# Reordering the first S5 scan: pairs of batches whose steps alternate, and two chains where a batch runs alone

## The chip, the core and the metric

The kernel runs on one core of one Trainium2 chip. The metric is the time of one execution on the device, in microseconds (us). Three runs of the kernel before took 1806.61, 1806.78 and 1822.71 us; the median is 1806.78 us. On the core, TensorE does the matmuls, VectorE and ScalarE the elementwise work, SyncE issues most of the DMAs, and GpSimd does almost nothing here. In the rows TensorE is PE (its weight loads are PEld), VectorE is DVE, ScalarE is ACT, SyncE is SP.

## The reference, cut to what matters

The model is four layers deep over 384 tokens: one sequence of 256 sample tokens and one of 128 prompt tokens, 1024 wide. Layers 0 and 3 are S5 layers, layer 1 is a pooling mixer, layer 2 is attention. An S5 layer projects the normed tokens to `u` and `z` (2048 wide each), drives 128 groups of 64 complex states with `u`, reads the states out, and ends with GELU, a gated linear unit and an output projection:

```
u, z = split(h @ w_in, 2)
for dirn in range(2):                      # forward and backward in time
    bu = einsum('blgc,gpc->blgp', ug, b_bar)
    _, states = associative_scan(_lin_rec, (a, bu), axis=1, reverse=(dirn == 1))
    y = y + einsum('blgp,gcp->blgc', states, c_mat).real
y = gelu(y)
y = y * sigmoid(y @ glu_w + glu_b)
out = (y * silu(z)) @ w_out
```

The scan is a linear recurrence `s[t] = a * s[t-1] + bu[t]` with complex numbers. The sample starts from given states, the prompt from zero, and the prompt's last states are an output.

## The kernel before, in words

**Tiling.** Four tokens are taken as one step of the recurrence, so the sample has 64 steps and the prompt 32. The 128 groups are done in four batches of 32 (`b` = 0 to 3). For one batch, the states of both directions lie on 128 partitions, and a tile `E` of 99 rows of 64 values holds them: rows 0 to 32 are the first half of the sample, rows 33 to 65 the prompt, rows 66 to 98 the second half of the sample. There are two such tiles, so batch 2 uses the tile of batch 0 and batch 3 that of batch 1.

**The scan** (`step`, from L1133). One step of one batch is three VectorE instructions, each of which needs the one before: a product `Pr` (state times the complex factor), a sum `R` of its parts, and an addition of `R` into the next row of `E`. In steps 0 to 31 one instruction covers the first half of the sample and the prompt together (`ns = 2`); here such a step is called wide, and its `Pr` writes 128x256. In steps 32 to 62 it covers the second half of the sample alone (`ns = 1`), a narrow step, whose `Pr` writes 128x128. Step 31 writes into row 66, where the second half of the sample begins. `Pr` and `R` have one buffer for even and one for odd batches.

**What surrounds the scan of a batch.** `u(b)` (L1074) multiplies the tokens with the weights for batch `b` on TensorE (L213), into three PSUM banks that VectorE transposes into a tile `U`; there are three `U` tiles, so `u(3)` writes the one of batch 0. `win(b, qq)` (L1099), four times a batch, makes a weight tile `W` (VectorE products `w`, transposes on TensorE at L910, copies on ScalarE), masks `U` on ScalarE (L1113), multiplies (L1122) and copies the result into `E` (L1125). `mats(q)` (L1222) makes the readout matrices `P` and `M` of a quarter (VectorE products `P`, `t`, TensorE L938, a round trip through DRAM). `out(b, qq)` (L1229) reads a quarter out: two large copies `Eq<-E` on ScalarE (L1185, L1188), matmuls (L1208, L1212), GELU, and a store to `yd`. `P` has four buffers. `z(q)` (L1086), 16 times, is a product for the gate path that only the end of the layer needs (TensorE L204). `fill` runs four pieces of the modulation of later layers (weights `adw` from DRAM, TensorE L99). `glu.early_y` and `glu.early_prod` begin the gated linear unit with what is ready.

**What sets the order.** `run` of `S5Body` (L1234) goes through the batches one after the other. For each it lists tasks by the step ahead of which they are to be written down (`at(step, task)`), then `rec` (L1156) writes down the 63 steps with the tasks between, then the four `out`. This is the order of writing. When the program is built, a planner gives every engine a fixed order of its own: it steps through estimated durations, and gives a free engine the first instruction in the order of writing whose inputs and buffers are ready in that estimate. On the chip every engine goes through its list in order and waits at semaphores. So the order of writing is a priority, not the order that runs. Layer 3 has a class of its own, `S5Skewed` (L1274), whose `phase` already alternates the second half of one batch with the first half of the next.

Of the kernel before, what the change touches and what calls it, by code (L numbers as in the profile page):

```python
# [9 lines left out]
F32 = mybir.dt.float32  # L10
# [1021 lines left out]
class S5Body:  # L1032
# [99 lines left out]

    def step(self, b, i):  # L1133


        n, sb, E = self.n, self.sb, self.Es[b % len(self.Es)]
        Tb = self.Tb[:, :, 32 * b:32 * b + 32].rearrange("p o a r -> p o (a r)")
        P = sb.tile([128, 256], F32, name="Pr", tag=f"Pr{b % 2}")
        R = sb.tile([128, 128], F32, name="R", tag=f"R{b % 2}")
        ns, x = (2, i) if i < 32 else (1, 34 + i)  # L1140
        at = lambda x, d=33: raw_ap(E, 64 * x, [[64 * d, ns], [1, 64]])
        P, R = P[:, :128 * ns].rearrange("p (o s a) -> p o s a", o=2, s=ns), R[:, :64 * ns].rearrange("p (s a) -> p s a", s=ns)
        yield n.tt(P, raw_ap(E, 64 * x, [[0, 2], [33 * 64, ns], [1, 64]]), Tb.unsqueeze(2).broadcast_to([128, 2, ns, 64]), OP.mult)
# [3 lines left out]
        yield n.tt(at(66, -1) if i == 31 else at(x + 1), R, at(x + 1), OP.add)  # L1147

# [6 lines left out]

    def rec(self, b, tasks):  # L1156

        self.begin(b)
        for i in range(63):
            for t in tasks.get(i, ()):  # L1160
                t()
            for _ in self.step(b, i):
                pass
        self.final(b)

# [65 lines left out]
    def run(self, h, fill, glu):  # L1231
# [7 lines left out]
        zs = list(range(16))  # L1239
        for b in range(4):  # L1240
            tasks = {}
            at = lambda i, f, *a: tasks.setdefault(i, []).append(lambda: f(*a))
            if b < 3:
                at(4, self.u, b + 1)
            for qq in range(4):
                if b < 3:
                    at(8 + 14 * qq, self.win, b + 1, qq)
                at(6 + 14 * qq, self.mats, 4 * b + qq)
            for k in range((3, 4, 3, 6)[b]):
                at(62, self.z, zs.pop(0))  # L1250
            if fill:
                for k in range((4, 3, 2, 1)[b]):
                    at(45, fill)
            if b == 3:
                for q in range(8):
                    at(min(62, 30 + 6 * q), glu.early_y, self.wq, q)
                for q in zs:
                    at(62, self.z, q)
                for q in range(2):
                    at(62, glu.early_prod, q)  # L1260
            self.rec(b, tasks)
            for qq in range(4):
                q = 4 * b + qq
                self.out(b, qq)
                if b == 3:
                    for k in range(2, 6):
# [7 lines left out]
class S5Skewed(S5Body):  # L1274

    def phase(self, f, tasks):

        if f < 4:  # L1280
            self.begin(f)
        for i in range(32):
            for t in tasks.get(i, ()):
                t()
            chains = ([self.step(f - 1, 32 + i)] if f and i < 31 else []) + ([self.step(f, i)] if f < 4 else [])
            for _ in range(3):
                for c in chains:
                    next(c)
        if f:
            self.final(f - 1)  # L1290

    def run(self, h, fill, glu):
# [7 lines left out]
        for f in range(5):  # L1300
# [14 lines left out]
            if f == 4:  # L1315
# [9 lines left out]
                for qq in (1, 2, 0):  # L1325
                    at(0, early, qq)
            self.phase(f, tasks)
            for qq in range(4 if f else 0):
# [205 lines left out]
```

## Time and profile before

The profiled execution took 1812.23 us, its span (first to last instruction) is 1810.4 us, and the mean granted TensorE clock is 0.963 of full speed.

| | busy us | share of the span |
|---|---|---|
| PE | 1686.1 | 93% |
| PEld | 1318.4 | 73% |
| DVE | 1254.9 | 69% |
| ACT | 978.3 | 54% |

The shares are averages over stages that differ. The chain of work that ended last lies 72% on PE, 9% on DVE, 9% on ACT and 6% on DMAs. The first S5 scan, which the change touches, begins at 92 us and the readout of its last batch ends at about 480 us.

### The profile page before, as it was taken

To read this page: it belongs to the slowest core of one execution; us is meant where nothing else is said; L and a number is where in the kernel's file an instruction comes from. 1 tells how busy PE (TensorE), PEld (TensorE's weight loads), DVE (VectorE), ACT (ScalarE), POOL (GpSimd) and SP (SyncE) were. 2 spreads that over 40 slices of the span, in tenths; PEclk is the share of its full clock that TensorE was granted. 3 is DMA by queue.
4 is the path that set the end of the run, shared out by engine and by line. 5 is a ranking of instruction groups with operands and counts; after the bars stand their busy time and mean duration, and the time that the engine had idled before them with its cause. 6 is when DMAs were issued, how large, how long until landed. Compare 5 with 4: busy or idle time off the path is not lost.

```text
span 1810.4 us, 29493 instructions
## 1 busy us (share of the span) xinstructions
PE 1686.1 (93%) x10928; PEld 1318.4 (73%) x10928; DVE 1254.9 (69%) x3149; ACT 978.3 (54%) x1588; POOL 5.4 (0%) x16
## 2 busy tenths in 40 slices
PE   4999999998999998999998999999899999899998
PEld 1464454654799977999887885657678778689986
DVE  7699876787476567888867737763439978656435
ACT  2653487636654455655546555642354777754322
POOL 0000000000000000000000000000000000000000
PEclk7999999997899998999998999999999999799999
DMA  8337767654577664655563566732567754567552
GB/s 311 98 119 240 228 182 220 195 180 137 166 252 231 193 205 135 188 162 163 179 218 113 186 205 229 239 127 82 181 226 226 227 182 140 166 232 213 172 165 72
DMA packets 174831, 334.30 MB, mean 185 GB/s; under 512 B 78528, under 2 KB 101856, under 8 KB 174688
## 3 DMA queue, kind: packets, MB, share of 16 engines
q1 hardware_dynamic: 165728, 319.84, 55.6%
q10 hardware_dynamic: 8960, 12.59, 2.1%
q8 instruction: 86, 1.41, 0.3%
q14 instruction: 57, 0.47, 0.1%
HBM read 279.54 MB, written 52.82 MB: 184 GB/s over the span
## 4 chain that ended last, share of the span: by engine, by line
PE 72%; DVE 9%; ACT 9%; DMA 6%; issue 3%; SPq 0%; ACTq 0%; DVEq 0%
PE acc L175 6%; PE acc L177 6%; PE acc L176 6%; PE sp L1122 4%; PE acc L829 4%; PE acc L830 4%; PE acc L831 4%; PE acc L213 3%; PE acc L159 3%; PE acc L160 3%; PE acc L161 3%; PE acc L204 3%; ACT Eq L1188 3%; DMA adw<-in_ada_w 2%; PE adps L99 2%
## 5 line engine op out<-in xcount | busy, mean ns | idle before, releaser
L51 DVE TENSOR_TENSOR wlo<-raw,whi 128x1024 fp32r<-128x1024 f32 (+2 forms) x234 | 281.2, 1204 | 246.3 <-ACT whi L138 229.0
L138 ACT CAST whi<-raw 128x1024 fp32r<-128x1024 f32 x246 | 257.6, 1050 | 315.2 <-PE acc L177 130.0
L51 DVE TENSOR_TENSOR Pr<-E,Tb 128x256 f32<-128x256 f32 (+1 forms) x504 | 173.9, 354 | 9.3 <-ACT E L1131 3.3
L159 PE MATMUL acc<-hh,whi 128*128 128x384 f32 x512 | 177.3, 347 | 0.2
L161 PE MATMUL acc<-hh,wlo 128*128 128x384 f32 x512 | 174.3, 340 | 0.3 <-DVE wlo L51 0.2
L160 PE MATMUL acc<-hl,whi 128*128 128x384 f32 x512 | 174.3, 340 | 0.0
L829 PE MATMUL acc<-y,whi 128*128 128x384 f32 x448 | 152.7, 345 | 8.1 <-ACT y L146 5.8
L831 PE MATMUL acc<-y,wlo 128*128 128x384 f32 x448 | 152.0, 340 | 1.0 <-DVE wlo L51 1.0
L830 PE MATMUL acc<-y,whi 128*128 128x384 f32 x448 | 152.7, 342 | 0.1
L175 PE MATMUL acc<-whi,ph 128*128 128x512 f32 x384 | 152.5, 397 | 0.0
L176 PE MATMUL acc<-wlo,ph 128*128 128x512 f32 x384 | 151.4, 394 | 0.0
L177 PE MATMUL acc<-whi,pl 128*128 128x512 f32 x384 | 151.3, 394 | 0.0
L51 DVE TENSOR_TENSOR E<-R,E 128x128 f32<-128x128 f32 (+1 forms) x504 | 123.1, 254 | 31.5 <-ACT E L1125 25.2
L51 DVE TENSOR_TENSOR R<-Pr 128x128 f32<-128x128 f32 (+1 forms) x504 | 123.7, 255 | 5.8
L159 PEld LDWEIGHTS acc<-hh,whi 128*128 128x128 f32 x512 | 97.1, 190 | 5.2 <-issue 2.0
L204 PE MATMUL acc<-h,raw 128*128 128x384 f32 x256 | 98.8, 516 | 0.0
L161 PEld LDWEIGHTS acc<-hh,wlo 128*128 128x128 f32 x512 | 96.8, 189 | 2.1 <-DVE wlo L51 0.9
L160 PEld LDWEIGHTS acc<-hl,whi 128*128 128x128 f32 x512 | 97.1, 190 | 1.0 <-issue 0.3
L99 PE MATMUL adps<-adw,scond 128*32 128x256 f32 x768 | 70.6, 422 | 27.7 <-DMA adw<-in_ada_w 27.3
L213 PE MATMUL acc<-raw,h 128*128 128x512 f32 x192 | 95.8, 617 | 0.0
L829 PEld LDWEIGHTS acc<-y,whi 128*128 128x128 f32 x448 | 84.6, 190 | 11.6 <-ACT y L146 7.1
L831 PEld LDWEIGHTS acc<-y,wlo 128*128 128x128 f32 x448 | 84.9, 190 | 2.2 <-DVE wlo L51 1.6
(285 smaller groups left out, 3261.6 us busy)
## 6 DMA issues: line engine op xcount, KB each, us to landing
adw<-in_ada_w SPq DMA_DIRECT2D x96, 512.0 KB
raw<-in_s_glu SPq DMA_DIRECT2D x64, 512.0 KB
raw<-in_s_wu SPq DMA_DIRECT2D x48, 512.0 KB
raw<-in_s_wz SPq DMA_DIRECT2D x40, 512.0 KB
raw<-in_s_wo SPq DMA_DIRECT2D x32, 512.0 KB
yq<-yd SPq DMA_DIRECT2D x64, 192.0 KB
lod<-wlo SPq DMA_DIRECT2D x24, 512.0 KB
wlo<-lod SPq DMA_DIRECT2D x24, 512.0 KB
```

The costliest lines, as they stand in the source:

```text
L51: return self.nc.vector.tensor_tensor(out=out, in0=a, in1=b, op=op)
L138: nc.scalar.copy(out=hi, in_=raw)
L159: nc.tensor.matmul(ps, h, xh[:, kk, :ncol], start=i == 0, stop=False)
L160: nc.tensor.matmul(ps, h, xl[:, kk, :ncol], start=False, stop=False)
L161: nc.tensor.matmul(ps, l, xh[:, kk, :ncol], start=False, stop=i == n - 1)
L175: nc.tensor.matmul(ps, xh[:, kk, xs], h, start=kk == 0, stop=False)
L176: nc.tensor.matmul(ps, xh[:, kk, xs], l, start=False, stop=False)
L177: nc.tensor.matmul(ps, xl[:, kk, xs], h, start=False, stop=kk == 2 * nu - 1)
L204: self.nc.tensor.matmul(ps, w[:, k * 128:(k + 1) * 128], x[:, k, :], start=k == 0, stop=k == 7)
L829: self.nc.tensor.matmul(ps, h, y[:, 0, k], start=u == 0 and k == 0, stop=False)
L830: self.nc.tensor.matmul(ps, h, y[:, 1, k], start=False, stop=False)
L831: self.nc.tensor.matmul(ps, l, y[:, 0, k], start=False, stop=u == 1 and k == 7)
```

## The change

`step` gets an argument `part`: with it, a first-half step covers the sample (`part` 0) or the prompt (`part` 1) alone, with `Pr` and `R` buffers of its own. `rec` goes, and `phase`, moved from `S5Skewed` up to `S5Body`, takes its place: it writes down 32 rounds in which the second half of one batch (`second`) and the first half of another (`first`) alternate instruction by instruction. Where there is no `second`, the first half is written as two alternating narrow chains. `S5Body.run` now has six phases: batch 0 alone (two chains), batches 0 and 1 as a pair, the second half of batch 1 alone (one chain), and the same for batches 2 and 3. The tasks are listed anew over 32 rounds a phase. `u(f + 1)` stands at the head of phases 0 to 2, so `u(3)` comes with the second half of batch 1 and no longer with the first half of batch 2. `mats` and `win` stand in the phases of one batch. The 16 `z` were placed 3, 4, 3, 6 over the batches and are placed 2, 4, 2, 2, 4, 2 over the phases; the ten `fill` were 4, 3, 2, 1 and are 2, 2, 2, 2, 1, 1. `S5Skewed` passes its batches to the same `phase` and writes down what it did before.

```diff
-    def step(self, b, i):
+    def step(self, b, i, part=None):
...
-        P = sb.tile([128, 256], F32, name="Pr", tag=f"Pr{b % 2}")
-        R = sb.tile([128, 128], F32, name="R", tag=f"R{b % 2}")
+        c = (b + (part or 0)) % 2
+        P = sb.tile([128, 256], F32, name="Pr", tag=f"Pr{c}")
+        R = sb.tile([128, 128], F32, name="R", tag=f"R{c}")
         ns, x = (2, i) if i < 32 else (1, 34 + i)
+        if part is not None:
+            ns, x = 1, i + 33 * part
...
-    def rec(self, b, tasks):
-
-        self.begin(b)
-        for i in range(63):
+    def phase(self, first, second, tasks):
+
+
+        if first is not None:
+            self.begin(first)
+        for i in range(32):
             for t in tasks.get(i, ()):
                 t()
-            for _ in self.step(b, i):
-                pass
-        self.final(b)
+            chains = [self.step(second, 32 + i)] if second is not None and i < 31 else []
+            if first is not None:
+                chains += [self.step(first, i)] if second is not None else [self.step(first, i, p) for p in range(2)]
+            for _ in range(3):
+                for c in chains:
+                    next(c)
+        if second is not None:
+            self.final(second)
...
-        for b in range(4):
+
+        for f, (first, second) in enumerate(((0, None), (1, 0), (None, 1), (2, None), (3, 2), (None, 3))):
             tasks = {}
-            at = lambda i, f, *a: tasks.setdefault(i, []).append(lambda: f(*a))
-            if b < 3:
-                at(4, self.u, b + 1)
+            at = lambda i, g, *a: tasks.setdefault(i, []).append(lambda: g(*a))
+            if f < 3:
+                at(0, self.u, f + 1)
+            mat, win = ((0, 1), None, (1, 2), (2, 3), None, (3, None))[f] or (None, None)
             for qq in range(4):
-                if b < 3:
-                    at(8 + 14 * qq, self.win, b + 1, qq)
-                at(6 + 14 * qq, self.mats, 4 * b + qq)
-            for k in range((3, 4, 3, 6)[b]):
-                at(62, self.z, zs.pop(0))
-            if fill:
-                for k in range((4, 3, 2, 1)[b]):
-                    at(45, fill)
-            if b == 3:
+                if mat is not None:
+                    at(2 + 7 * qq, self.mats, 4 * mat + qq)
+                if win is not None:
+                    at(4 + 7 * qq, self.win, win, qq)
+            for k in range((2, 4, 2, 2, 4, 2)[f]):
+                at(31, self.z, zs.pop(0))
+            for k in range((2, 2, 2, 2, 1, 1)[f]):
+                at(24, fill)
+            if f == 5:
                 for q in range(8):
-                    at(min(62, 30 + 6 * q), glu.early_y, self.wq, q)
+                    at(min(31, 4 + 4 * q), glu.early_y, self.wq, q)
...
-            self.rec(b, tasks)
+            self.phase(first, second, tasks)
+            if second is None:
+                continue
             for qq in range(4):
-                q = 4 * b + qq
-                self.out(b, qq)
+                q = 4 * second + qq
+                self.out(second, qq)
```

## Rows read from the trace of the kernel before

**Rows 1.** Busy time by stretch: start:end, length, each engine's busy us (xcount), clock, DMA.

```profile
92.00:155.00 63.00, 62.24 (x653) 38.63 (x649) 58.17 (x146) 39.82 (x81) 0.00 (x0) 1.00 0.46 146
155.00:206.00 51.00, 47.17 (x232) 18.15 (x236) 46.16 (x212) 3.48 (x10) 0.00 (x0) 1.00 0.82 261
206.00:284.00 78.00, 73.20 (x741) 44.54 (x733) 52.93 (x156) 67.91 (x85) 0.15 (x1) 1.00 0.63 192
284.00:352.00 68.00, 63.95 (x576) 33.92 (x576) 55.52 (x147) 43.54 (x64) 0.15 (x1) 1.00 0.67 204
352.00:392.00 40.00, 39.98 (x277) 22.19 (x278) 36.36 (x170) 8.80 (x20) 0.00 (x0) 1.00 0.73 241
392.00:453.00 61.00, 49.06 (x314) 29.01 (x312) 42.55 (x148) 43.05 (x45) 0.00 (x0) 0.75 0.38 115
453.00:480.00 27.00, 23.23 (x173) 18.12 (x172) 15.98 (x21) 20.80 (x20) 0.70 (x1) 0.81 0.51 137
```

**Rows 2.** Timeline of DVE, 167 to 168 us: start, duration, what.

```profile
167.03 0.42 DVE L51 TENSOR_TENSOR Pr<-E,Tb 128x256 f32<-128x256 f32 x1
167.37 0.22 DVE L51 TENSOR_TENSOR E<-R,E 128x64 f32<-128x64 f32 x1
167.50 0.28 DVE L51 TENSOR_TENSOR R<-Pr 128x128 f32<-128x128 f32 x1
167.70 0.29 DVE L51 TENSOR_TENSOR Pr<-E,Tb 128x128 f32<-128x128 f32 x1
167.91 0.28 DVE L51 TENSOR_TENSOR E<-R,E 128x128 f32<-128x128 f32 x1
168.11 0.22 DVE L51 TENSOR_TENSOR R<-Pr 128x64 f32<-128x64 f32 x1
168.24 0.42 DVE L51 TENSOR_TENSOR Pr<-E,Tb 128x256 f32<-128x256 f32 x1
```

**Rows 3.** Timeline of DVE, 116 to 117 us, first half of batch 0.

```profile
115.82 0.42 DVE L51 TENSOR_TENSOR Pr<-E,Tb 128x256 f32<-128x256 f32 x1
116.28 0.29 DVE L51 TENSOR_TENSOR R<-Pr 128x128 f32<-128x128 f32 x1
116.61 0.29 DVE L51 TENSOR_TENSOR E<-R,E 128x128 f32<-128x128 f32 x1
116.94 0.43 DVE L51 TENSOR_TENSOR Pr<-E,Tb 128x256 f32<-128x256 f32 x1
```

**Rows 4.** Timeline of DVE, 447 to 448 us, second half of batch 3.

```profile
447.05 0.29 DVE L51 TENSOR_TENSOR Pr<-E,Tb 128x128 f32<-128x128 f32 x1
...
447.90 0.29 DVE L51 TENSOR_TENSOR Pr<-E,Tb 128x128 f32<-128x128 f32 x1
```

**Rows 5.** Timeline of ACT, 300 to 364 us; in brackets idle time before and its releaser.

```profile
302.43 2.94 ACT L1188 COPY Eq<-E 64x1536 f32<-64x1536 f32 x1
...
316.96 0.62 ACT L1113 ACTIVATE U<-U,masks 128x384 f32<-128x384 f32 x1 [8.36 <-DVE U L1084]
...
362.49 0.48 ACT L1125 COPY E<-sp 128x384 f32<-128x384 f32 x1 [0.32 <-PE sp L1122]
```

**Rows 6.** Groups of DVE, 352 to 392.6 us (first row), then 392.6 to 413.7 us.

```profile
L51 DVE TENSOR_TENSOR Pr<-E,Tb 128x256 f32<-128x256 f32 x24 | 10.0, 418 | 0.0
...
L51 DVE TENSOR_TENSOR Pr<-E,Tb 128x256 f32<-128x256 f32 x8 | 3.4, 422 | 0.2
L51 DVE TENSOR_TENSOR P<-C,Lf 128x512 f32<-128x512 f32 x4 | 2.6, 688 | 7.1 <-PE tp L1212 4.4 <-PE ad L1212 2.7
```

**Rows 7.** Busy time of L204, L213, L99 in turn, 92 to 352 us: PE, PEld, ...

```profile
92.00:352.00 260.00, 50.30 (x128) 21.57 (x128) 1.00 0.64 198
...
92.00:352.00 260.00, 66.18 (x136) 23.27 (x136) 1.00 0.64 198
...
92.00:352.00 260.00, 42.63 (x488) 11.27 (x488) 1.00 0.64 198
```

More of the change, by code (lines that the diff above doesn't have):

```diff
@@ L1146, in step @@
         yield n.tt(rv.rearrange("p s a o -> p o s a"), pv[:, :, :, :, 0], pv[:, :, :, :, 1], OP.add)
-        yield n.tt(at(66, -1) if i == 31 else at(x + 1), R, at(x + 1), OP.add)
+        yield n.tt(at(66, -1) if i == 31 and not part else at(x + 1), R, at(x + 1), OP.add)
     def final(self, b):
@@ L1239, in run @@
         zs = list(range(16))
-        for b in range(4):
+        for f, (first, second) in enumerate(((0, None), (1, 0), (None, 1), (2, None), (3, 2), (None, 3))):
             tasks = {}
-            at = lambda i, f, *a: tasks.setdefault(i, []).append(lambda: f(*a))
-            if b < 3:
-                at(4, self.u, b + 1)
+            at = lambda i, g, *a: tasks.setdefault(i, []).append(lambda: g(*a))
+            if f < 3:
+                at(0, self.u, f + 1)
+            mat, win = ((0, 1), None, (1, 2), (2, 3), None, (3, None))[f] or (None, None)
             for qq in range(4):
-                if b < 3:
-                    at(8 + 14 * qq, self.win, b + 1, qq)
-                at(6 + 14 * qq, self.mats, 4 * b + qq)
-            for k in range((3, 4, 3, 6)[b]):
-                at(62, self.z, zs.pop(0))
-            if fill:
-                for k in range((4, 3, 2, 1)[b]):
-                    at(45, fill)
-            if b == 3:
+                if mat is not None:
[7 more added lines that the diff above has]
+            if f == 5:
                 for q in range(8):
-                    at(min(62, 30 + 6 * q), glu.early_y, self.wq, q)
-                for q in zs:
-                    at(62, self.z, q)
+                    at(min(31, 4 + 4 * q), glu.early_y, self.wq, q)
                 for q in range(2):
-                    at(62, glu.early_prod, q)
-            self.rec(b, tasks)
+                    at(31, glu.early_prod, q)
+            self.phase(first, second, tasks)
+            if second is None:
+                continue
             for qq in range(4):
-                q = 4 * b + qq
-                self.out(b, qq)
-                if b == 3:
+                q = 4 * second + qq
+                self.out(second, qq)
+                if f == 5:
                     for k in range(2, 6):
@@ L1274 @@
 class S5Skewed(S5Body):
[L1278 to L1290, printed above, removed]
     def run(self, h, fill, glu):
@@ L1326, in run @@
                     at(0, early, qq)
-            self.phase(f, tasks)
+            self.phase(f if f < 4 else None, f - 1 if f else None, tasks)
             for qq in range(4 if f else 0):
```

## The prediction

> **What bounds the kernel now.** I read the shares of busy time first and set them aside: DVE's 69% is a mean over stages with different limits, and the change touches one stage, the first S5 scan. I then cut that stage where the form of DVE's `Pr` instructions changes, wide to narrow [rows 1]. The seven stretches are: first half of batch 0 (92 to 155); the end of it, then second half of 0 beside first half of 1 (to 206); second half of 1 (to 284); first half of 2 (to 352); second half of 2 beside first half of 3 (to 392); the rest of 3 (to 453); the last readout (to 480). The reader should see three things. TensorE is busy 246.6 of the first 260 us, so until 352 us it has 13.4 us to give. DVE is 92% busy in the first stretch and 91% in the second. From 392 us on no engine is full, and the granted clock falls to 0.75: there a chain of waits sets the time.
>
> Next I read DVE's timeline. In the pair stretch the steps of two batches already alternate one instruction at a time [rows 2], though they were written down batch after batch: the planner had pulled them together. So most of what the change writes down is what ran already, and its worth must come from what it moves.
>
> **The price of a step.** In the pair [rows 2], start to start, a wide step takes 0.34 + 0.20 + 0.20 = 0.74 us of DVE and a narrow one 0.13 + 0.21 + 0.13 = 0.47, a round 1.21. With nothing between, a wide step takes 116.94 - 115.82 = 1.12 us [rows 3] and a narrow one 0.85 [rows 4]: each instruction then waits about 0.13 us for the one before. The Trainium skill ("VectorE: DVE Perf Modes", The DRAIN you can't avoid) says that a next instruction cannot issue until the pipe has emptied, chained or not. By that sentence, alternating chains would win nothing; the rows of the pair speak against it, since there an instruction of the other chain starts 0.13 to 0.34 us after one that runs 0.22 to 0.42 us.
>
> **Part a, two chains where a batch is alone (batches 0 and 2).** 32 wide steps become 64 narrow ones, 96 more instructions each time. Two alternating narrow chains take 2 x 0.47 = 0.94 us a step, 30.1 us in all. The wide steps took between 32 x 0.74 = 23.7 (every gap filled by other DVE work) and 32 x 1.12 = 35.8 us (none filled). So each batch costs between -5.7 and +6.4 us. The `mats` and `win` products run there, and DVE is busy 58.2 of 63 and 55.5 of 68 us [rows 1], nearer to filled: I take +2.5 each, **+5** together; ends -11 and +13.
>
> **Part b, `u(3)` earlier.** Batch 3's `win` needs the `E` tile of batch 1, whose last `Eq` copy ended at 305.4, and `U` of `u(3)`. ACT then stood idle 8.36 us for DVE's transposes of `u(3)` and masked `U` only at 316.96; the last `E` copy of `win(3)` ended at 363.0 [rows 5], 11 us after the pair stretch began. So that stretch held 31 narrow steps but only 24 wide ones; 8 were left over, and ran alone behind two waits [rows 6]. With `u(3)` at the head of phase 2, TensorE does it while ACT makes the readout copies of batch 0, and `win(3)` can start some 8 to 11 us earlier. The pair is then 32 full rounds, 38.7 us, plus the 3.6 us that DVE idles there now [rows 1], 42.3 instead of 40.6, and 8 x 1.12 = 9.0 us after it go: net -7.3, rounded to **-8** because the second half of batch 2 no longer runs partly alone. It is 0 if `win(3)` stays late, and -16 if the 7.1 us of waits for free `P` buffers [rows 6] go as well; I keep those, as readout copies set them.
>
> **Part c, `z` and `fill`.** Up to 352 us the 128 records of L204 [rows 7] are 8 of the 16 `z` (8 matmuls of two records each), 50.3 / 8 = 6.3 us apiece. The new list has 10 in its first four phases: 12.6 us more for an engine that idles 13.4 us there. `fill`: 488 records of L99 [rows 7] are 30 pieces of 16, and the new list has 32 there, 2 x 16 x 0.087 = 2.8 us more. Both stand last in their phases, so they mostly slip into idle time: **+3**, ends 0 and +15. What they leave after 392 us saves nothing, TensorE not being the bound there.
>
> **Part d, the two middle stretches.** In 206 to 352 us DVE idles 37.6 us [rows 1]. Part of it is in-order waiting behind a TensorE that is full with `u(3)`: three `u` are 144 records, some missing from the trace, at 66.18 / 136 = 0.487 us [rows 7], 23.4 us each. Taken out of 284 to 352 us, this lets readout, transposes and `win` follow faster. TensorE's work in the two stretches stays the same, so the gain ends at its idle time there, 4.8 + 4.1 = 8.9 us. I take **-6**; ends -9 and, if `u(3)` delays what now stands behind it, +18.6 (second rival).
>
> **Edits at nothing.** After 392 us `mats(12)` to `(15)` now stand among narrow steps of batch 3 instead of wide ones; their waits for `P` remain and hold up the chain queued behind them on DVE as before (cover gone: one more wait, 4.4 us [rows 6]). SP issues the four weight loads of `u(3)` and two of `z` earlier. In phase 1 the DMA engines are 0.82 busy at 261 GB/s [rows 1]; two `z` weights of 0.5 MB are 4 us there, hidden behind DVE's scan, and cost up to 4 us if TensorE waits for them in order. Waits on buffers: batch 1's chain and the prompt's chain of batch 0 now share the odd `Pr`, and each is free again one instruction later, 0.2 us. Layer 3 writes down what it did.
>
> **Sum.** +5 - 8 + 3 - 6 = -6 us. The sum is made on an execution of 1812.2 us (span 1810.4), which would become 1806; the median of the runs lies 5.4 us lower, at 1806.8, and becomes **1801**. A change of 1%, 18 us, is about what a measurement of this kernel can tell from none.
>
> **The rivals.**
> 1. *The planner did it all already.* For it: the alternation is there [rows 2], and 8 `z` had run by 352 us [rows 7] where the list had 3 + 4 written by then. Then `win(3)` is as late as now, and only the split counts: +5, 1812 us. Against it: a task's place sets its priority, and `u(3)` moves by half a batch.
> 2. *Slower: TensorE's queue before the readout of batch 0.* `u(3)` is now written ahead of `win(2)`, and four `z` fall into the pair phase, where TensorE has 3.8 us left [rows 1]. If their tail runs after 206 us, 23.4 us of `u(3)` stand in front of `win(2)` with 4.8 us of idle time to absorb them: +18.6, with a and c +27, 1834 us. It decides once batch 2's last `E` copy comes later than some 10 us after 284. For it: TensorE is 94% busy there. Against it: the copies of batch 0's readout leave TensorE waiting at the start of that stretch anyway, and `z` filled the time.
> 3. *Larger gain.* Parts b and d at their ends, and a and c free: -16 - 9 = -25, 1782 us. For it: DVE idles 37.6 us in the middle and waits 7.1 us at the end, and ACT is 44 of 68 us busy beside it. Against it: TensorE has no such reserve.
> 4. *No overlap of chains*, as the page says: the 64 narrow steps take 64 x 0.85 = 54.4 us instead of some 27.6 in each of two phases, +54, less b: 1853 us. The rows of the pair all but exclude it.
>
> **Chances.** Forecast 0.43, rival 1 0.17, rival 2 0.15, rival 3 0.23, rival 4 0.02. Faster by over 1% (below 1789): rival 3 mostly, and the lower end of the forecast, 0.26. Slower by over 1% (above 1825): most of rivals 2 and 4, 0.14. Within 1%: 0.60. The range goes from just below rival 3 to just below rival 2, 1777 to 1828. The forecast's own range is 1790 to 1810.
>
> **What would show it.** Part a: single-batch stretches with 128x128 `Pr` only, two chains 0.94 us a round, DVE busier there. Part b: the last `E` copy of batch 3 before the first half of batch 2 ends, 32 wide beside 31 narrow steps in the second pair, and no 8.36 us wait of ACT on the transposes. Part c: at least 150 records of L204 before the second pair. Part d: less DVE idle time between the first pair and the second. The prediction is wrong in its core if `win(3)` still ends within the second pair, or if the stretch after the first pair grows beyond 78 us.

## The result, and the profile after

Nine runs of the changed kernel took 1825.3 to 1834.1 us, median 1829.6; nine of the kernel before on the same chip took 1806.6 to 1822.7, median 1812.1. The ratio is 1.0096, with a 95% interval from 1.0070 to 1.0121: slower by about 1%, where the prediction said 0.3% faster. The profiled span grew by 13.9 us, from 1810.4 to 1824.3. In the changed file the readout copies are L1195 and L1198, the readout matmuls L1218 and L1222; `u` (L213), `z` (L204) and `fill` (L99) keep their lines.

The page of after, its sums by engine, and behind it the same line of before:

```profile
span 1824.3 us, 29791 instructions
PE 1690.7 (93%) x10928; PEld 1319.7 (72%) x10928; DVE 1258.5 (69%) x3437; ACT 979.1 (54%) x1588; POOL 5.4 (0%) x16
...
PE 1686.1 (93%) x10928; PEld 1318.4 (73%) x10928; DVE 1254.9 (69%) x3149; ACT 978.3 (54%) x1588; POOL 5.4 (0%) x16
```

TensorE has 4.6 us more busy time than before and 9.3 us more without work, DVE 3.6 us more busy time. Such totals do not say where the loss arose; the stretches do. The counts set one thing right: DVE has 288 instructions more (3437 for 3149), three times 96 and not twice. `phase` splits every first half that has no partner, so also that of batch 0 in layer 3, which `S5Skewed` used to write down as one wide chain. From the first product of layer 3's `u(0)` to the end of the span it takes 498.2 us after and 496.5 before, so this third split is at most a small part of the 13.9 us.

After, busy time by stretch, cut as in [rows 1] where the form of `Pr` changes (columns as there):

```profile
92.00:154.00 62.00, 61.58 (x616) 36.84 (x611) 58.02 (x235) 38.44 (x78) 0.00 (x0) 1.00 0.49 138
154.00:194.00 40.00, 39.45 (x195) 17.63 (x193) 38.05 (x183) 4.07 (x10) 0.00 (x0) 1.00 0.70 223
194.00:297.00 103.00, 94.10 (x798) 52.11 (x798) 63.54 (x189) 71.09 (x89) 0.15 (x1) 0.98 0.62 192
297.00:367.00 70.00, 66.24 (x664) 40.87 (x662) 57.78 (x230) 47.78 (x75) 0.15 (x1) 1.00 0.64 196
367.00:405.00 38.00, 36.55 (x218) 17.38 (x217) 34.99 (x176) 5.92 (x12) 0.00 (x0) 1.00 0.84 269
405.00:470.00 65.00, 44.46 (x314) 28.91 (x313) 46.37 (x153) 43.88 (x47) 0.00 (x0) 0.63 0.43 137
470.00:497.00 27.00, 25.27 (x210) 19.80 (x209) 14.17 (x24) 19.96 (x18) 1.59 (x1) 1.00 0.53 151
```

Against [rows 1] the first pair ends 11 us shorter (40 for 51), the stretch behind it is 25 longer (103 for 78), then +2, -2 and +4. What follows 470 us is 3 us shorter than what followed 453. With -1 for the first stretch that is +14, the whole difference.

The later cuts do not stand at quite the same events in both. By events, from the `Pr` of DVE and the copies of ACT: the first half of batch 2 ends at 368.4 us (351.8 before), its second half at 410.8 (392.8), the first half of batch 3 at 413.0 (414.1), its second half at 472.5 (452.4), and the last GELU of the readout at 502.5 (491.1; the 480 of the text above is the end of its copies). So after is 16.6 us late when the first half of batch 2 ends, makes up 5.2 us by the end of the last readout, and loses 2.5 behind it, 1.7 of them from layer 3's first product on.

Of the two signs that the prediction named as wrong in its core, one is plain: the stretch after the first pair is beyond 78 us. The other is there by a hair: `win(3)` ends at 369.8 us, and the first step of batch 3 begins at 369.1 (363.0 and 352.4 before).

Which work fills these stretches is seen from `z` and `u` alone. First `z` (L204), then `u` (L213), each in three stretches: first pair, the stretch behind it, the first half of batch 2. The kernel before:

```profile
155.00:206.00 51.00, 14.30 (x38) 6.46 (x38) 1.00 0.82 261
206.00:284.00 78.00, 20.48 (x54) 9.28 (x54) 1.00 0.63 192
284.00:352.00 68.00, 6.93 (x16) 2.58 (x16) 1.00 0.67 204
...
155.00:206.00 51.00, 23.79 (x48) 8.06 (x48) 1.00 0.82 261
206.00:284.00 78.00, 4.32 (x8) 1.21 (x8) 1.00 0.63 192
284.00:352.00 68.00, 20.03 (x40) 6.70 (x40) 1.00 0.67 204
```

After, in the same order:

```profile
154.00:194.00 40.00, 10.70 (x30) 5.46 (x31) 1.00 0.70 223
194.00:297.00 103.00, 22.22 (x58) 9.62 (x58) 0.98 0.62 192
297.00:367.00 70.00, 23.06 (x62) 10.37 (x60) 1.00 0.64 196
...
154.00:194.00 40.00, 22.00 (x48) 8.71 (x48) 1.00 0.70 223
194.00:297.00 103.00, 22.05 (x48) 8.64 (x48) 0.98 0.62 192
297.00:367.00 70.00, 0.00 (x0) 0.00 (x0) 1.00 0.64 196
```

`u(3)` did move: 20.0 us left the third stretch and 17.7 came to the second. But the third stretch did not get shorter, because 16.1 us of `z` took the place. Over the three stretches `z` has 56.0 us instead of 41.7, some 14 more, and by these cuts the second pair starts 15 us later, at 367 for 352.

What the order does at the first readout, after, on TensorE (start, duration, what; some lines left out):

```profile
196.10 1.56 PE L204 MATMUL acc<-h,raw 128*128 128x384 f32 x4
...
212.70 2.85 PE L204 MATMUL acc<-h,raw 128*128 128x384 f32 x8
215.97 0.64 PE L99 MATMUL adps<-adw,scond 128*32 128x256 f32 x8 [0.42 <-DMA adw<-in_ada_w]
216.54 0.46 PE L1218 MATMUL tp<-U,M 128*128 128x96 f32 x2
...
247.02 11.43 PE L213 MATMUL acc<-raw,h 128*128 128x512 f32 x26
...
304.38 2.20 PE L204 MATMUL acc<-h,raw 128*128 128x384 f32 x6
306.84 0.64 PE L99 MATMUL adps<-adw,scond 128*32 128x256 f32 x8 [0.26 <-DMA adw<-in_ada_w]
307.41 0.46 PE L1218 MATMUL tp<-U,M 128*128 128x96 f32 x2
```

and on ACT the first copy of the readout of batch 0, the first of batch 1, and the last of batch 1:

```profile
197.03 2.95 ACT L1195 COPY Eq<-E 64x1536 f32<-64x1536 f32 x1 [4.24 <-DVE E L51]
...
251.70 2.86 ACT L1195 COPY Eq<-E 64x1536 f32<-64x1536 f32 x1 [4.07 <-DVE E L51]
...
328.51 2.81 ACT L1198 COPY Eq<-E 64x1536 f32<-64x1536 f32 x1
```

Batch 0's first pair of copies ended at 202.9, and its matmuls came at 216.5, behind the last of the four `z`, which was done at 216. Batch 1's copy began at 251.7 and its matmuls at 307.4, 56 us later (273 and 282 before): `u(3)`, `win(2)` and more `z` stood ahead. So its last copy ended at 331.3 (305.4 before, [rows 5]).

TensorE's busy time from 400 to 500 us, before, then after, each from its own trace:

```profile
400.00:500.00 100.00, 87.29 (x602) 62.66 (x601) 57.49 (x149) 65.53 (x74) 1.59 (x1) 0.80 0.48 142
```

```profile
400.00:500.00 100.00, 77.48 (x576) 53.42 (x574) 65.54 (x201) 66.19 (x67) 1.59 (x1) 0.76 0.49 154
```

After has 9.8 us more without work here, of 9.3 in the whole span; between like events, from the end of batch 2's first half to the last GELU, it is 8.0 us (23.7 for 15.7). By 400 us 14 of its 16 `z` were done (10 before), so they were no longer there to fill the waits of the last scan.

### The profile page after: what moved, and what is told of

It reads as the page before. It is cut to its first block, busy times and chain, and to the rows that moved or that the text cites. A ratio compares the mean times of both kernels' runs of the same rounds, so it can differ in the third digit from the quotient of the medians.

```text
span 1824.3 us, 29791 instructions
## 1 busy us (share of the span) xinstructions
PE 1690.7 (93%) x10928; PEld 1319.7 (72%) x10928; DVE 1258.5 (69%) x3437; ACT 979.1 (54%) x1588; POOL 5.4 (0%) x16
## 4 chain that ended last, share of the span: by engine, by line
PE 54%; DVE 9%; ACT 6%; DMA 3%; issue 2%; SPq 0%; ACTq 0%; DVEq 0%
PE acc L175 6%; PE acc L176 6%; PE acc L177 6%; PE acc L829 4%; PE acc L831 4%; PE acc L830 3%; PE acc L159 3%; PE acc L160 3%; PE acc L161 3%; DVE wlo L51 2%; PE sp L1122 2%; PE sp L730 2%; ACT Eq L1198 2%; PE sp L729 2%; PE acc L762 1%
## 5 line engine op out<-in xcount | busy, mean ns | idle before, releaser
L51 DVE TENSOR_TENSOR Pr<-E,Tb 128x128 f32<-128x128 f32 (+1 forms) x600 | 177.1, 319 | 15.7 <-PE sp L439 11.7
L51 DVE TENSOR_TENSOR E<-R,E 128x64 f32<-128x64 f32 (+1 forms) x600 | 126.5, 235 | 31.4 <-ACT E L1125 27.3
L51 DVE TENSOR_TENSOR R<-Pr 128x64 f32<-128x64 f32 (+1 forms) x600 | 127.0, 236 | 4.1
L99 PE MATMUL adps<-adw,scond 128*32 128x256 f32 x768 | 73.2, 428 | 27.2 <-DMA adw<-in_ada_w 26.0
L204 PE MATMUL acc<-h,raw 128*128 128x384 f32 x256 | 97.0, 506 | 0.0
L213 PE MATMUL acc<-raw,h 128*128 128x512 f32 x192 | 92.0, 610 | 0.0
```

Source lines behind the costliest of these rows:

```text
L51: return self.nc.vector.tensor_tensor(out=out, in0=a, in1=b, op=op)
L204: self.nc.tensor.matmul(ps, w[:, k * 128:(k + 1) * 128], x[:, k, :], start=k == 0, stop=k == 7)
```

## The experiments

Each kernel was timed in five rounds beside the kernel before. That kernel's medians in the seven sets were 1809.4 to 1815.1 us, so the ratios are what to compare; 0.1% is 1.8 us. A trace is one execution, and those of a1, b3, c1, d1, d2 and e1 lie 5 to 9 us from their medians. The expectations name theories by letters. **A**: non-urgent work stands in TensorE's queue ahead of critical products. **B**: the split and its 192 (in fact 288) more DVE instructions cost it all. **C**: early `u(3)` hurts only in the changed list. **D**: early `u(3)` costs by itself. **A2**: what counts is the `z` between a readout's copies and its matmuls. **E**: the first pair cannot hold both `u(2)` and four `z`. **F**: no rule about one stretch. **G**: the delayed `u(2)` becomes the late one.

| run | base | edit | median us | ratio to before (95%) |
|---|---|---|---|---|
| after | | | 1829.6 | 1.0096 (1.0070 to 1.0121) |
| a1 | after | `u(3)` late | 1816.5 | 1.0027 (1.0006 to 1.0048) |
| a2 | after | `z` as before | 1819.8 | 1.0052 (1.0034 to 1.0071) |
| a3 | after | both | 1810.1 | 0.9991 (0.9979 to 1.0004) |
| a4 | after | no split | 1826.1 | 1.0083 (1.0067 to 1.0099) |
| b1 | before | `u(3)` early | 1813.9 | 1.0014 (0.9999 to 1.0029) |
| b2 | before | split | 1811.6 | 1.0001 (0.9987 to 1.0014) |
| b3 | before | `z` as after | 1805.1 | 0.9952 (0.9936 to 0.9969) |
| a5 | after | `z` later, `u(3)` late, no split | 1833.7 | 1.0121 (1.0100 to 1.0142) |
| c1 | after | `z` clear of the readouts | 1827.9 | 1.0102 (1.0075 to 1.0128) |
| c2 | after | `z` written behind them | 1832.8 | 1.0127 (1.0105 to 1.0150) |
| c3 | after | c2 and `u(3)` late | 1835.2 | 1.0147 (1.0123 to 1.0170) |
| b4 | before | `z` written behind them | 1839.8 | 1.0168 (1.0145 to 1.0190) |
| d1 | after | `u(2)`, `u(3)` late | 1799.1 | 0.9938 (0.9915 to 0.9961) |
| d2 | after | d1, `z` as before | 1808.6 | 0.9983 (0.9965 to 1.0001) |
| d3 | after | d1, no split | **1794.8** | 0.9905 (0.9884 to 0.9927) |
| e1 | after | `u(2)` late, `u(3)` early | 1821.9 | 1.0049 (1.0028 to 1.0071) |
| e2 | before | `u(2)`, `win(2)` late, `z` as after | 1819.1 | 1.0036 (1.0014 to 1.0057) |
| e3 | before | the whole task list of d3 | 1800.3 | 0.9922 (0.9902 to 0.9942) |

**One part undone (a1 to a4).** In a1, `u(3)` goes back to the first half of batch 2:

```diff
-            if f < 3:
-                at(0, self.u, f + 1)
+            if f in (0, 1, 3):
+                at(0, self.u, {0: 1, 1: 2, 3: 3}[f])
```

> The changed kernel (1829.6 us median) with u(3) moved from the head of phase 2 back to the head of phase 3. Theory A, TensorE's queue (the four z of phase 1 stand in front of the readout matmuls of batch 0, u(3) in front of win(2)): u(3) ran on TensorE from 247 to 258 us between the readout of batch 0 and the first W transposes of batch 2, so without it the last E copy of batch 2 comes about 11 us earlier (286 instead of 297); win(3) gets later again, so 1818 to 1825 us. Theory B, the split into two chains costs it all (192 more DVE instructions): no change, 1826 to 1833 us.

In a2 the `z` are placed nearly as before; a3 has both edits.

```diff
-            for k in range((2, 4, 2, 2, 4, 2)[f]):
+            for k in range((2, 1, 4, 1, 2, 6)[f]):
```

> The changed kernel with the 16 z placed 2, 1, 4, 1, 2, 6 over the phases (3 ahead of the first readout, as before, instead of 6). Theory A: the readout matmuls of batch 0 start some 12 us earlier (204 instead of 216.5 us), win(2) ends some 10 us earlier, 1815 to 1823 us. Theory B: no change, 1826 to 1833 us.

> Both moves at once: u(3) at the head of phase 3 and z placed 2, 1, 4, 1, 2, 6. Theory A: both queues in front of batch 2 are gone, win(2) ends at 275 us or so, and the time is that of the kernel before or a little less, 1800 to 1813 us. Theory B: 1826 to 1833 us.

In a4 a batch that runs alone keeps its wide steps, the one in layer 3 too:

```diff
-                chains += [self.step(first, i)] if second is not None else [self.step(first, i, p) for p in range(2)]
+                chains += [self.step(first, i)]
```

> The changed kernel with the first halves of batches 0 and 2 as one wide chain again (96 DVE instructions fewer in each of two phases), all else kept. Theory A with the price of part a: 5 us less, 1822 to 1829 us. Theory B: the whole loss goes, 1808 to 1815 us.

Measured: a1 gave back 0.69%, a2 0.44%, a3 1.05%, which is all of it. So the two placements are the loss, and about additive; B falls. What else the change moved comes to nothing in sum. a2's interval just touches that of after, and a1 came out 1.5 us below its range. The split alone is 0.13%, its intervals overlapping.

**One part done alone in the old list (b1 to b3).** b1 puts `u(3)` at step 32 of batch 1, b2 runs even batches as two narrow chains in their first half (with `step` as in the change; layer 3 keeps its own `phase`), b3 places `z` as the change does:

```diff
-            if b < 3:
+            if b < 2:
                 at(4, self.u, b + 1)
+            if b == 1:
+                at(32, self.u, 3)
```

> The kernel before with only u(3) moved, from step 4 of batch 2 to step 32 of batch 1, where the change has it. Theory A (work put ahead of the critical products in TensorE's order costs, and u(3) early is the larger part): slower by 6 to 13 us, 1817 to 1824 us, with the last E copy of batch 2 later than 284 us. Rival theory C (u(3) early hurts only because the rest of the changed list, pairs and phases, leaves it no room; in the old list it helps batch 3, as my part b had it): 1800 to 1808 us, the last E copy of batch 3 earlier than 355 us.

```diff
...
-            for _ in self.step(b, i):
-                pass
+            chains = [self.step(b, i, p) for p in range(2)] if b % 2 == 0 and i < 32 else [self.step(b, i)]
+            for _ in range(3):
+                for c in chains:
+                    next(c)
```

> The kernel before with only the split: the first halves of batches 0 and 2 as two alternating narrow chains. Theory A with part a: 0 to 6 us slower, 1811 to 1817 us. Theory B (192 more DVE instructions cost much): 1820 us or more. Theory C: the same as A here.

```diff
-            for k in range((3, 4, 3, 6)[b]):
+            for k in range((6, 2, 6, 2)[b]):
```

> The kernel before with the z placed 6, 2, 6, 2 over the batches, as many ahead of each readout as in the changed kernel. Theory A: the readout matmuls of batch 0 wait behind z on TensorE, 5 to 10 us slower, 1816 to 1821 us. Theory C: within 3 us, since in the old list the planner runs z in the idle time of TensorE.

Measured: b1 costs 0.14%, with an interval that just reaches zero; in its trace batch 3's last `E` copy comes later, not earlier (375.9 us for 363.0), as in after, though batch 2's first half ended earlier (337 for 352). The split costs nothing here. And the `z` placement that costs 0.44% in after gains 0.48% in the old list. In b3 the `z` ran in the pair (done at 169, 175, 184 and 192 us) and `u(2)` behind them, its last transpose at 240 us for 200 before. b1 and b3 lie outside both of their expectations. A count of early `z` can thus not be the rule; what they displace matters.

**Fewer `z` early (a5).** a4's and a1's edits, and `z` still later:

```diff
-            for k in range((2, 4, 2, 2, 4, 2)[f]):
+            for k in range((2, 0, 3, 1, 2, 8)[f]):
```

> The changed kernel with u(3) at the head of phase 3, wide steps where a batch is alone, and z placed 2, 0, 3, 1, 2, 8. Theory A: still less stands ahead of the first two readouts, and the two z more at the end run while TensorE is half idle there: 1798 to 1807 us. If z at the end hold up the first products of the gated linear unit in the same way: 1808 to 1818 us. Theory B: as the kernel before, 1808 to 1815 us, from the missing split alone.

It missed: 1833.7. Batch 3's readout copies began at 448 us, 25 earlier than after, but its matmuls at 486, behind eight `z` that were done from 449 to 486. Work put off too long stands ahead of the last readout.

**Is it the `z` between a readout's copies and its matmuls (c1 to c3, b4)?** c1 has no `z` at the places ahead of readouts 0 and 1:

```diff
-            for k in range((2, 4, 2, 2, 4, 2)[f]):
+            for k in range((2, 1, 0, 5, 2, 6)[f]):
```

> The changed kernel, u(3) early as in it, with z placed 2, 1, 0, 5, 2, 6: none written in the phase ahead of the readout of batch 1. Theory A2 (what costs is z standing on TensorE between a readout's copies on ACT and its matmuls; in the changed kernel the first copy for batch 1 starts at 252 us and the first matmul at 308, after two z): the gap falls to under 10 us, win(3) ends before 355 us, and the time is 1803 to 1815 us. Theory D (u(3) early costs by itself, because its 23 us stand in front of win(2) and the readout of batch 1 comes behind win(2)): the gap stays over 30 us, 1816 to 1826 us.

c2 writes the `z` of a phase with a readout behind the four `out`; c3 also has `u(3)` late (a1's edit); b4 does the same to batches 0 to 2 of the kernel before.

```diff
             for k in range((2, 4, 2, 2, 4, 2)[f]):
-                at(31, self.z, zs.pop(0))
+                if second is None:
+                    at(31, self.z, zs.pop(0))
...
+            for k in range((2, 4, 2, 2, 4, 2)[f]):
+                self.z(zs.pop(0))
```

> The changed kernel with the z of phases 1, 2, 4 and 5 written behind the readout that ends the phase instead of ahead of it; their number a phase is kept, u(3) early. Theory A2: both readouts' matmuls follow their first copies by under 10 us, 1803 to 1815 us. Theory D: the readout of batch 0 does, that of batch 1 does not, 1815 to 1824 us.

> As the last one, and u(3) at the head of phase 3. Theory A2: about the same as the last, within 5 us of it. Theory D: 1803 to 1812 us, 8 us or more faster than the last.

> The kernel before with the z of batches 0 to 2 written behind the readout of their batch. There the first matmul follows the first copy by 6 to 9 us already in all four readouts, so by A2 and D alike there is nothing to win: within 5 us of the kernel before, 1805 to 1816 us. If the z placed 6, 2, 6, 2 were faster there because they ran early in idle time of TensorE, this one is slower, 1812 to 1820 us.

From the first copy to the first matmul that reads one took 6 us at the readout of batch 0 in all four (20 after), and 8 to 20 us at that of batch 1 (56 after). Yet c1 and c2 are no faster than after, their intervals overlapping it, and c3 and b4 are slower. A2 falls. D falls in this form too: c1's gap is 8 us where D had over 30, and c3, with `u(3)` late, is 2.4 us slower than c2 (the intervals overlap) where D had it 8 faster. b4 missed both of its ranges. In c1 four `z` were done at 333 to 353 us instead, ahead of `win(3)`; in b4 TensorE idled 30 us between 92 us and the second pair, where before idled 13.

**`u(2)` and `u(3)` each one phase later (d1 to d3).**

```diff
-            if f < 3:
-                at(0, self.u, f + 1)
+            if f in (0, 2, 3):
+                at(0, self.u, {0: 1, 2: 2, 3: 3}[f])
```

> The changed kernel with u(2) and u(3) each one phase later (u at the head of phases 0, 2 and 3); z as in the change. Theory E (the first pair is 40 us long and TensorE has 39.5 us of work in it; u(2), some 23 us, and four z, 25 us, don't both fit, so z runs on into the readout of batch 0): with u(2) gone from the pair, all four z end before batch 0's readout copies begin, u(2) runs beside these copies, and batch 1's readout matmuls follow its copies by less than 15 us. It gives 1804 to 1812 us, at least 5 us less than with u(3) late alone (1816.5). Rival F (no rule about one stretch: whatever order TensorE's full list has up to 400 us, moving a product only moves the queueing): within 3 us of 1816.5. Rival G (u(2) becomes the late one: win(2) now waits for it, as it waits in the first phases for nothing): batch 2's last E copy comes after 296 us, and the time is 1825 or more.

> As the run before, but z placed 2, 1, 4, 1, 2, 6 over the phases, near where the kernel before has them. Theory E: the first pair then holds 1 z and no u, TensorE idles in it some 15 us and this time is missing later: 1812 to 1822 us, slower than the run before by 5 or more. Rival F: within 3 us of the kernel with u(3) late and z as before (1810). Rival A (fewer z early is always better): 1802 to 1808.

> The first of these runs with the sample and the prompt in one wide chain where a batch runs alone. Part a of the prediction put the split at +5 us, ends -11 and +13; in the changed list taking it out gained 3.5 us. If that holds here: 3 to 5 us faster than the first of these runs, 1800 to 1808 by theory E. If the split is free where TensorE is the bound (as in the old list, 0.0): the same within 2 us.

d1 took 1799.1, even below E's 1804; of the time before, 1.58% less than after and 0.89% less than a1. F and G fall by it. d2 is slower than d1 by 0.45%, as E said, but faster than E's 1812 (F's 1810 held it too), and not for lack of work in the pair: TensorE is busy 39.9 of 41 us there, because the planner pulled `u(2)` back into it (last transpose at 199 us). d3, with all three splits undone, gains another 0.33% on d1, about what part a had for two, though the two intervals overlap; it lies below its own range.

d1, `z` (L204), then `u` (L213), in the first pair, the stretch behind it and the first half of batch 2:

```profile
157.00:196.00 39.00, 27.04 (x74) 12.57 (x72) 1.00 0.86 282
196.00:284.00 88.00, 8.76 (x20) 3.07 (x20) 0.90 0.58 174
284.00:356.00 72.00, 9.88 (x24) 3.90 (x24) 1.00 0.57 174
...
157.00:196.00 39.00, 2.73 (x6) 0.98 (x6) 1.00 0.86 282
196.00:284.00 88.00, 22.30 (x43) 7.85 (x42) 0.90 0.58 174
284.00:356.00 72.00, 22.05 (x48) 8.63 (x48) 1.00 0.57 174
```

Each stretch holds one large product: the `z` fill the pair, where TensorE has nothing critical; `u(2)` runs among the readout matmuls of batch 0, just ahead of the `win(2)` that needs it; `u(3)` the same a batch later. The stretch behind the first pair is 88 us, for 103. (This execution's clock fell to 0.90 there and it took 6.8 us more than d1's median, so the row understates it.) The first readout, d1, ACT's second copy and TensorE's first matmul:

```profile
201.91 2.87 ACT L1198 COPY Eq<-E 64x1536 f32<-64x1536 f32 x1
...
204.83 0.54 PE L1222 MATMUL tp<-Eq,P 128*64 128x96 f32 x6 [1.47 <-ACT Eq L1198]
```

The matmul now waits 1.47 us for the copy, where in after the readout's first matmul (L1218, ahead of those that read a copy) came 13.6 us after the copy (216.5 less 202.9).

**Which of the two, and what the phases are worth (e1 to e3).** e1 takes only `u(2)` out of the pair and leaves `u(3)` early, though in the middle of phase 2 and not at its head:

```diff
-            if f < 3:
-                at(0, self.u, f + 1)
+            for i, b in (((0, 1),), (), ((0, 2), (16, 3)), (), (), ())[f]:
+                at(i, self.u, b)
```

> The changed kernel with u(2) at the head of phase 2 (out of the first pair) and u(3) early still, in the middle of phase 2 between the second and the third part of win(2); z as in the change. It is the fourth corner: u(2) and u(3) early 1829.6, u(3) alone late 1816.5, both late 1799.1. If the overfilled first pair is the larger part of the loss: the pair holds four z alone as in the best runs, u(2) runs beside batch 0's readout copies, and only u(3)'s price is left, 10 to 13 us over both late: 1808 to 1813. If u(3) in phase 2 is what loses, with u(2) only adding to the queue: u(2) and u(3) now stand together in the 70 to 80 us after the first pair, batch 1's readout matmuls start 30 us or more after its first copy, and it takes 1820 to 1832.

e2 and e3 are the kernel before, written batch after batch. e2 moves `u(2)`, `win(2)` and `z`:

```diff
-                at(4, self.u, b + 1)
+                at(32 if b == 1 else 4, self.u, b + 1)
...
-                    at(8 + 14 * qq, self.win, b + 1, qq)
+                    at(34 + 7 * qq if b == 1 else 8 + 14 * qq, self.win, b + 1, qq)
...
-            for k in range((3, 4, 3, 6)[b]):
+            for k in range((6, 2, 6, 2)[b]):
```

> The kernel before, in its old form (batch after batch, no phases, no split), with u(2) and the four win(2) written in the second half of batch 1 and z 6, 2, 6, 2: nearly the order of the best run. If the order of TensorE's work in and behind the first pair is all that counts and the rewriting into phases gives nothing: 1792 to 1800, as the best run (1794.8). If b3 (before with z 6, 2, 6, 2: 1805.1, where u(2) already came behind the z in the first pair) has all that the old form can give: 1802 to 1807, and the phases are worth some 8 us.

e3 takes over d3's whole list, `mats`, `fill` and the early gated unit too, phases 0 and 1 on the two halves of batch 0, phase 2 on the second half of batch 1, and so on:

```diff
+            for f, o in (((0, 0), (1, 32)), ((2, 32),), ((3, 0), (4, 32)), ((5, 32),))[b]:
+                if f in (0, 2, 3):
+                    at(o, self.u, {0: 1, 2: 2, 3: 3}[f])
...
+                        at(o + 2 + 7 * qq, self.mats, 4 * mat + qq)
...
+                        at(o + 4 + 7 * qq, self.win, win, qq)
+                for k in range((2, 4, 2, 2, 4, 2)[f]):
+                    at(min(62, o + 31), self.z, zs.pop(0))
```

> The kernel before, still written down batch after batch (no alternating chains, no split), with the whole task list of the best run (u, mats, win, z, fill and early GLU at the same steps of the same halves; u(2) in the second half of batch 1, u(3) in the first half of batch 2). If the list of tasks is all that counts, and e2 (1819) was slow because its mats stood elsewhere: 1792 to 1800, as the best run (1794.8). If writing the chains as pairs is worth something by itself, because the first half of the next batch is then planned beside the second half of this one and not behind it and its readout: 1806 to 1820, near e2.

With e1 the four corners are, but for that difference: both early +0.96%, `u(3)` late +0.27%, `u(2)` late +0.49%, both late -0.62%. `u(3)` is the dearer one (0.69 and 1.11%), `u(2)` worth 0.47 and 0.89%, and each helps more with the other done. e1 is what its second statement said: the copy of batch 1 began at 269 us and its matmuls at 311. So E's full pair is one part of the cause, not the larger one.

e2 was slower than both of its expectations, e3 all but as fast as d3 (0.9922 and 0.9905, the intervals overlap; 0.3 us above its first range). The list of tasks is therefore nearly all of it, and writing the chains as pairs is worth 0.2% or nothing: in e3 the planner alternates the chains by itself, 37 wide `Pr` beside 26 narrow ones from 155 to 200 us, as it did in [rows 2]. What makes e2 lose 1.1% to e3 lies in the places of `mats`, `win(1)`, `win(3)`, `fill` and the early gated unit and in smaller moves of `u` and `z`; no run separates these.

d3, the fastest, from 92 us to the second pair (columns as in [rows 1]):

```profile
92.00:346.00 254.00, 241.42 (x2104) 134.25 (x2105) 214.75 (x663) 152.85 (x236) 0.30 (x2) 1.00 0.62 190
```

## Why the prediction was wrong, step by step

The forecast of 1801 stood on 1806.8, the median of three runs; nine put the kernel before at 1812.1, so 5.3 of the 28.6 us between 1801 and 1829.6 belong to that base. The rest is in the sum: up to the end of batch 2's first half it had +5, +3 and -6 (parts a, c, d), and the trace shows +16.6.

**The premise that failed: "until 352 us it has 13.4 us to give".** From 92 us to the second pair TensorE was without work 13.4 of 260 us before, 13.6 of 275 after (61.58 + 39.45 + 94.10 + 66.24 = 261.4 busy), 12.6 of 254 in d3 (241.4 busy). The idle time did not shrink when work was added; 14.8 us more work took 15 us more time. What is left idle is made of waits at fixed places of the list (in after for readout copies, for `adw`, for a DVE product), and filler written down elsewhere did not fall into them. In these three kernels the time to the second pair is thus TensorE's work ahead of it and some 13 us. Over all runs the idle part is 10 to 21 us, but 30 in b4, so this is a pattern here and not a constant.

**Part c** is where that enters the sum: "they mostly slip into idle time", +3, ends 0 and +15. Two `z` more were priced rightly, 12.6 us by the list and 14.3 in the rows; they cost the upper end. The other side of the same account is the 9.8 us without work after 400 us: the prediction had written that what the `z` leave there "saves nothing", and did not ask what would fill the waits there.

**Part b** was right about `win(3)` and wrong about what that is worth. `u(3)` was done by 258.5 us, and ACT's mask of `U` no longer waits 8.36 us [rows 5]; the line of these masks from 294 to 371 us in after (nanoseconds least, median, longest; first and last start), which has no idle time ahead of it, and the last `E` copy:

```profile
L1113 ACT ACTIVATE U<-U,masks x8: 597/614/617, 295.1 to 359.5; 128x384 f32<-128x384 f32 x8
...
369.33 0.48 ACT L1125 COPY E<-sp 128x384 f32<-128x384 f32 x1 [0.90 <-PE sp L1122]
```

That copy ends later than before (369.8 for 363.0): `u(3)` ahead of `win(2)` delays batch 1's readout, which releases the `E` tile, from 305.4 to 331.3 us, and TensorE did not do `u(3)` beside the copies of batch 0; the `z` were there. But it ends 0.7 us after batch 3's first step, where before it ended 10.5 after, so relative to the pair it is the forecast 8 to 11 us earlier. The pair is what was forecast too, 32 wide steps beside 31 narrow, in the 44 us from 369 to 413; before, the 32 took the 62 us from 352.3 to 414.2 (first after, then before):

```profile
L51 DVE TENSOR_TENSOR Pr<-E,Tb 128x256 f32<-128x256 f32 x32 | 13.3, 416 | 0.0
L51 DVE TENSOR_TENSOR Pr<-E,Tb 128x128 f32<-128x128 f32 x31 | 8.8, 283 | 0.0
...
L51 DVE TENSOR_TENSOR Pr<-E,Tb 128x256 f32<-128x256 f32 x32 | 13.4, 419 | 0.2
```

So batch 3's first half ended 1.1 us earlier than before, though it began 16.7 us later. The 31 narrow steps of its second half then took 57.4 us for 37.7 (their `Pr`, and the `P` of `mats` among them; after, then before):

```profile
L51 DVE TENSOR_TENSOR Pr<-E,Tb x31: 278/291/293, 415.1 to 472.2; 128x128 f32<-128x128 f32 x31
L51 DVE TENSOR_TENSOR P<-C,Lf 128x512 f32<-128x512 f32 x8 | 5.4, 686 | 10.0 <-PE tp L1222 7.2 <-PE ad L1222 2.7
...
L51 DVE TENSOR_TENSOR Pr<-E,Tb x31: 281/292/294, 414.8 to 452.1; 128x128 f32<-128x128 f32 x31
L51 DVE TENSOR_TENSOR P<-C,Lf 128x512 f32<-128x512 f32 x2 | 1.3, 688 | 1.7 <-PE tp L1212 1.7
```

What failed is "8 x 1.12 = 9.0 us after it go". The wide steps left over before ran while `mats(12)` to `(15)` waited for `P`, which the readout of batch 2 releases. That readout begins when batch 2's second half ends, at 411.9 us for 393.7, and from its first copy to the end of batch 3's scan it takes 60.6 us after and 58.7 before. With no wide steps left the same waits stand among the narrow ones. The prediction had noted "cover gone" among its edits at nothing, and did not take it off part b.

**Part d** said that without `u(3)` the stretch from 284 to 352 would let readout and `win` follow faster. The planner filled the room with `z` (23.1 us for 6.9). In the changed list the runs show this as a pattern: in each of its four pairs that differ in the place of `u(3)` alone, the early one has 5 to 11 us more of `z` between 92 us and the end of batch 2's first half, and that end comes 5 to 15 us later (in brackets): after 65.1 and a1 55.2 us of `z` (368, 360), a2 58.7 and a3 48.4 (355, 347), c2 60.3 and c3 54.9 (364, 359), e1 64.7 and d1 53.5 (367, 353). Room made in the list draws filler into it. The later end is not always a loss: c2 is not slower than c3. And in the old list it is the other way: b1 has 51.6 and before 50.1 us of `z`, and in b1 that half ended 15 us earlier (337, 352).

**Rival 2** had the place and the price: `u(3)` ahead of `win(2)` behind a full pair, +18.6, decided by a last `E` copy of batch 2 more than 10 us after 284. It came at 296.1, `u` has 17.7 us more in that stretch, and the stretch was 25 us longer. It missed that the first pair would be 11 us shorter (batch 0's first half was done by then: 29 wide `Pr` stand there, for 37), so that its +27 stands against 17.5 measured (1829.6 less 1812.1), and its chance of 0.15 was too low. The reason given against it, that `z` filled the wait for the copies anyway, was what made it worse: they ran 13.6 us past it.

**Part a** was right in its price of a round. Two narrow chains take 0.95 us a round (110.07 to 111.02), 0.94 by the rows; after, DVE in the first half of batch 0:

```profile
110.07 0.48 DVE L51 TENSOR_TENSOR Pr<-E,Tb 128x128 f32<-128x128 f32 x2
110.48 0.35 DVE L51 TENSOR_TENSOR R<-Pr 128x64 f32<-128x64 f32 x2
110.75 0.35 DVE L51 TENSOR_TENSOR E<-R,E 128x64 f32<-128x64 f32 x2
111.02 0.48 DVE L51 TENSOR_TENSOR Pr<-E,Tb 128x128 f32<-128x128 f32 x2
```

The split costs 0.33% in d1 against d3 and 0.13% in after against a4, 6 and 2 us with the third batch in layer 3, and nothing in the old list, where layer 3 is not split. So +5 is at the upper end of what was measured, and no pair of intervals is apart. The prediction's "Layer 3 writes down what it did" was wrong by one split.

**Rival 4** rested on a sentence of the Trainium skill ("VectorE: DVE Perf Modes", The DRAIN you can't avoid). These rows speak against it as [rows 2] did: the second chain's instruction starts within the first one's time. The Trainium skill (same page, Two Vector instructions with no wait between them) has instructions start early unless a condition holds them, which the prediction left out; the trace agrees with that.

**Rival 1** was true of the alternation, which the planner makes by itself (e3), and false of the placement.

## What to carry to other kernels

That an engine is 95% busy does not mean that the other 5% can be given away: see where its idle time lies before pricing added work at nothing, and price work moved ahead of a critical product at its full length. Filler belongs in the stretch where the engine waits on something else and nothing critical is behind it; here the pair of d1 took 39 us with 27.0 us of `z` in it, and in after 22.2 us of `z` ran in the stretch behind it, much of it ahead of critical products. When a product is moved earlier, follow what now stands behind it to the buffer that it releases, and ask what the planner will put into the place left free. Before steps that ran late are counted as saved, ask whether they filled a wait that stays. And before a rewrite is credited or blamed, run its task list in the old form (e3), since here that was nearly the whole gain.

## What the runs showed of the hardware

In after, from 405 to 470 us, TensorE was busy 44.5 of 65 us and its granted clock 0.63, so it ran at the lower level for much of that time; a readout matmul took 368 ns. d1 kept `z` for that stage (21.5 us of them from 393 to 458 us; after has 3.7 from 405 to 470), with a granted clock of 0.95 there and 246 ns for the same matmul. Lines of L1222 in 405 to 470 us (columns: least, median and longest ns, first and last start), first after, then d1:

```profile
L1222 PE MATMUL tp<-Eq,P x64: 364/368/423, 417.7 to 440.1; 128*64 128x96 f32 x64
```

```profile
L1222 PE MATMUL tp<-Eq,P x96: 246/246/297, 406.8 to 468.6; 128*64 128x96 f32 x96
```

The Trainium skill ("TensorE: Matmul & The Clock Gate", Part 1) says that the clock follows how busy the engine has been; the two stretches agree. So filler may do something beside its own work, by keeping the clock up for the critical matmuls around it. No run here tests that by itself (the two kernels differ in more than the `z`), and what it is worth was not measured; the stretch is 65 us in both.
